# Laid-out inputs, a scan in contiguous fours and a joined 512-column stream in a two-layer attention and state-space trunk

## The chip, the cores and the metric

The kernel runs on one core of one Trainium2 chip. The metric is device time in microseconds (us) of one execution: the median of the runs shown. The engines are called PE (TensorE), PEld (its weight loads), DVE (VectorE), ACT (ScalarE), POOL (GpSimd) and SP (SyncE, which here only issues transfers).

## What is computed

The input x has 256 positions of 2048 numbers. Two layers, each:

```
h    = rmsnorm(x, pre_norm_g)
proj = h @ w_in                       # 2048 -> 6144: q, k, v, z_att, u, z_ssm
o_att = rmsnorm(diff_attention(q, k, v), subln_g) * (1 - lam_init) * silu(z_att)
y     = s5_ssm(u)                     # 64 groups of 16 channels, 64 complex states each,
                                      # h[t] = A h[t-1] + B u[t],  y = Re(C h) + D u
g     = gelu(y) @ w_glu               # 1024 -> 2048: value and gate
o_ssm = g_val * sigmoid(g_gate) * silu(z_ssm)
mix   = concat(o_att, o_ssm) @ w_out  # 2048 -> 2048
x     = x + rmsnorm(mix, post_norm_g)
```

Attention has 8 heads with two softmax maps each, a chunk-causal mask and a T5 bias table. All tensors are float32.

## The kernel before, in words

**Products in three parts.** A float32 weight tile `raw` (128 x 1024) is split into `hi`, the value rounded to fp32r by ACT (`emit_hi`, line 227), and `lo = raw - hi`, the rest, by DVE (`emit_lo`, line 245). The activations are split in the same way into `hthi` and `htlo` (later `mxhi`, `mxlo` and `ghi`, `glo`). One product is then three matmuls: hi on hi, hi on lo, lo on hi.

**Half steps.** All weights of a layer are cut into 72 chunks, in the order u (the first half as `U4`, four k groups at a time for all four column blocks; the second half as `u`), q, k, v and z_att in turns, z_ssm, w_glu, w_out. Each chunk is two half steps (hs) of one 512 KB weight tile, 288 half steps in all. The loop at line 1174 does for each half step: issue the load of half step hs + 6 (`emit_dma`, SP's queue, five buffers), start what is due (`hooks`, line 1081), round the weights of hs + 2 on ACT, let the running generators go on one step (`run_first`), compute lo of hs + 2 on DVE with other DVE work filled around it, issue the matmuls of hs (`main`, line 981), and let generators waiting for accumulators go on (`run_second`). In u, q and k the weights are the stationary operand and the activations stream, 256 columns: 24 matmuls a half step. In v, z, w_glu and w_out the activations are stationary and 512 weight columns stream: 12 matmuls a half step.

**The planner.** Each DVE helper adds an estimated cost (`cost`, line 100) to a sum. What is left of a half step's budget (`BUDS`, `BUDL`, `CAP`, lines 1141 and 1229) is given to `fill` (line 213), which takes operations from a queue (`weave`): parameters, discretisation (`z_ops`, `g_ops`), the scan.

**Start of layer 1** (the first layer; the code's l = 0). x is loaded by positions in four column pieces (line 1150), transposed on PE (`build`, line 634, four transposes for two k groups, one call per half step up to the sixth), scaled by the norm's gain and split. The sum of squares is made by ACT from x (`rstd_gen`, line 650); the row scale comes after the product, as `rbc`, when u, q, k are evacuated (`evac`, line 919).

**State space.** `prep_gen` (line 485) loads B with 8 DMAs (line 496) and C with 4 (line 501), transposes C with 16 PE transposes into `psc`, and builds the matrices for four time steps at once (z, wi, gc, the Toeplitz block t0). It runs for layer 1 from half step 2 and for layer 2 beside layer 1's w_glu stage. u goes to DRAM and comes back as U, four steps to a row (`u_store`, `u_load`, lines 680 and 684), `s_gen` (line 718) makes the inputs of 64 blocks, `scan_ops` (line 753) runs 62 sequential steps of four 128 x 64 operations on DVE, and `y_gen` (line 766) makes y, gelu and its split into `ghi`, `glo`, one fourth at a time.

```
    def scan_ops(l):                                              # line 753
        for s in range(2, 64):
            yield mul(t1, H[:, :, :, s - 1], ar) + SC
            yield mul(t2, H[:, ::-1, :, s - 1], ai)
            yield tt(t1, t1, H[:, :, :, s], ALU.add) + SC
            yield tt(H[:, :, :, s], t1, t2, ALU.add) + SC
...
            for kk in range(8):                                   # line 1014, u, q, k
                mm(o, hv[:, kk], S["hthi"][:, k], k == 0, False)
                mm(o, hv[:, kk], S["htlo"][:, k], False, False)
                mm(o, lv[:, kk], S["hthi"][:, k], False, k == 15)
```

At the very start `warm` (line 1135) keeps PE busy with products of ones until the first data are there: one call of six, one of `W1` = 1 and one of `W2` = 3.

Of the kernel before, what the change touches and what calls it, by code (L numbers as in the profile page):

```python
# [26 lines left out]
SC = 70  # L27
Y0 = (80, 77)
W1 = 1
W2 = 3  # L30
TB = 38
PG = 1
CAP = 1500.0
RES = 0.0
# [6 lines left out]
F0 = 7  # L41
EB = 400
# [5 lines left out]
NA = 2  # L48
TPS = ([(0, 1024), (1024, 1024)], [(0, 512), (512, 768), (1280, 768)])
# [7 lines left out]

@with_exitstack
def hybrid_trunk(ctx: ExitStack, tc, x, rel_bias, pre_norm_g, post_norm_g, w_in, lambda_q1, lambda_k1,
                 lambda_q2, lambda_k2, subln_g, ssm_a_re, ssm_a_im, ssm_log_dt, ssm_b_re, ssm_b_im,  # L60
                 ssm_c_re, ssm_c_im, ssm_d, w_glu, w_out, onehot, out):
# [80 lines left out]
    a4s = cp.tile([128, 2, 64], F32, name="a4s")  # L142
    cf = cp.tile([128, 2, 64], F32, name="cf")
# [17 lines left out]
    w_in_v = [w_in[l].rearrange("(k p) c -> p k c", p=128) for l in range(2)]  # L161
    w_glu_v = [w_glu[l].rearrange("(k p) c -> p k c", p=128) for l in range(2)]
    w_out_v = [w_out[l].rearrange("(k p) c -> p k c", p=128) for l in range(2)]
    chunks = []
    for l in range(DEPTH):
        chunks += [(l, "U4", n) for n in range(4)] + [(l, "u", b) for b in range(4, 8)]
        for seg in ("q", "k"):
            chunks += [(l, seg, b) for b in range(8)]
        for n in range(2):
            for seg in ("v", "za"):  # L170
                chunks += [(l, seg, 4 * n + j) for j in range(4)]
        for seg, n in (("zs", 8), ("glu", 8), ("out", 16)):
            chunks += [(l, seg, b) for b in range(n)]

# [5 lines left out]
    def emit_dma(hs):  # L180
        if hs >= 2 * NCH:
            return
        l, seg, b = chunks[hs // 2]
        h = hs % 2
        t = wp.tile([128, 1024], F32, tag="raw", name="raw")
        raw[hs] = t
        if seg in ("u", "q", "k"):
            c0 = COL[seg] + 128 * b
            src = w_in_v[l][:, 8 * h:8 * h + 8, c0:c0 + 128]
        elif seg == "glu":  # L190
            k0, c0 = 4 * (b % 2) + 2 * h, 1024 * (1 - b // 2 % 2) + 512 * (b // 4)
            src = w_glu_v[l][:, k0:k0 + 2, c0:c0 + 512]
        elif seg == "U4":
            src = w_in_v[l][:, 4 * b + 2 * h:4 * b + 2 * h + 2, COL["u"]:COL["u"] + 512]
        elif seg == "out":
            k0, c0 = 4 * (b % 4) + 2 * h, 512 * (b // 4)
            src = w_out_v[l][:, k0:k0 + 2, c0:c0 + 512]
        else:
            k0, c0 = 4 * (b % 4) + 2 * h, COL[seg] + 512 * (b // 4)
            src = w_in_v[l][:, k0:k0 + 2, c0:c0 + 512]  # L200
        tv = t.rearrange("p (k c) -> p k c", k=src.shape[1])
        if hs == 0:
            for kk in range(2):
                SY.dma_start(out=tv[:, kk], in_=src[:, kk])
        else:
            SY.dma_start(out=tv, in_=src)
# [20 lines left out]
    def emit_hi(hs, halves=False):  # L227
# [10 lines left out]
        else:  # L238
            hi = sp.tile([128, 1024], F32R, tag="hi", name="hi")
        for p in range(1 + halves):  # L240
            c = slice(512 * p, 512 * p + 512) if halves else slice(0, 1024)
            act(hi[:, c], raw[hs][:, c], AF.Copy)
        split[hs] = (hi, None)

    def emit_lo(hs, budget, halves=False):
        if hs >= 2 * NCH:
            return
        src, hi = raw.pop(hs), split[hs][0]
# [236 lines left out]
    def prep_gen(l, slots):  # L485
# [16 lines left out]
        for _ in range(4 if l else 6):  # L502
            yield
# [787 lines left out]
```

## Time and profile before

| | |
|---|---|
| median of 3 runs | 926.35 us (925.54 to 928.47) |
| profiled execution, its own time | 926.7 us |
| its span, first to last instruction | 924.9 us |
| granted TensorE clock, mean | 0.994 |
| DMA | 187,892 packets, 177.21 MB, mean 192 GB/s |

The span is 1.8 us shorter than the execution's own time. Busy time of PE is modelled from pipelined matmuls, so the spacing of matmuls says more than its share. Layers are numbered 1 and 2 here; the code has l = 0 and 1.

### The profile page before, as it was taken

To read this page: it belongs to the slowest core of one execution; us is meant where nothing else is said; L and a number is where in the kernel's file an instruction comes from. 1 tells how busy PE (TensorE), PEld (TensorE's weight loads), DVE (VectorE), ACT (ScalarE), POOL (GpSimd) and SP (SyncE) were. 2 spreads that over 40 slices of the span, in tenths; PEclk is the share of its full clock that TensorE was granted. 3 is DMA by queue.
4 is the path that set the end of the run, shared out by engine and by line. 5 is a ranking of instruction groups with operands and counts; after the bars stand their busy time and mean duration, and the time that the engine had idled before them with its cause. 6 is when DMAs were issued, how large, how long until landed. Compare 5 with 4: busy or idle time off the path is not lost.

```text
span 924.9 us, 17644 instructions
## 1 busy us (share of the span) xinstructions
PE 907.7 (98%) x6722; PEld 795.1 (86%) x6722; DVE 683.5 (74%) x1606; ACT 488.1 (53%) x881; POOL 17.2 (2%) x26
## 2 busy tenths in 40 slices
PE   9999999999999999999999999999999999999995
PEld 8999999888888788887889999997888788888884
DVE  4898686999995756877877449999966566665564
ACT  6643384455465667444468443335565655644451
POOL 3000000000000000000000000000000000000001
PEclk9999999999999999999999999999999999999998
DMA  9988656855654497576656866965556346665852
GB/s 303 209 231 244 185 165 172 278 158 168 184 155 137 126 232 243 171 249 201 215 173 193 230 175 168 246 187 165 163 156 183 115 137 203 197 210 168 291 183 91
DMA packets 187892, 177.21 MB, mean 192 GB/s; under 512 B 42550, under 2 KB 131184, under 8 KB 186912
## 3 DMA queue, kind: packets, MB, share of 16 engines
q1 hardware_dynamic: 187456, 175.96, 64.3%
q8 instruction: 53, 0.87, 0.4%
q14 instruction: 31, 0.25, 0.1%
q0 software_dynamic: 352, 0.13, 0.1%
HBM read 168.44 MB, written 7.88 MB: 191 GB/s over the span
## 4 chain that ended last, share of the span: by engine, by line
PE 87%; DVE 5%; ACT 3%; DMA 2%; SPq 1%; issue 1%; DVEq 0%; ACTq 0%
PE ac L113 79%; DVE lo L116 2%; DMA xt<-in_x_dram 1%; PE lga L113 1%; PE psy L113 1%; PE pss L113 1%; PE po L113 1%; SPq L496 1%; PE psw L97 1%; PE acu L113 1%; ACT junk L134 1%; DMA raw<-in_w_glu_dram 1%; ACT hi L134 1%; DMA raw<-in_w_in_dram 1%; ACT y L134 0%
## 5 line engine op out<-in xcount | busy, mean ns | idle before, releaser
L134 ACT ACTIVATE hi<-raw 128x1024 fp32r<-128x1024 f32 (+1 forms) x282 | 297.8, 1056 | 357.3 <-PE ac L113 272.2
L116 DVE TENSOR_TENSOR lo<-raw,hi 128x512 fp32r<-128x512 f32 (+1 forms) x401 | 359.8, 901 | 105.5 <-ACT hi L134 104.3
L113 PE MATMUL ac<-hthi,hi 128*128 128x256 f32 x736 | 211.7, 288 | 0.3 <-ACT hi L134 0.3
L113 PE MATMUL ac<-htlo,hi 128*128 128x256 f32 x736 | 209.4, 285 | 0.8 <-DVE htlo L123 0.5
L113 PE MATMUL ac<-hthi,lo 128*128 128x256 f32 x736 | 209.1, 284 | 0.6 <-DVE lo L116 0.5
L113 PE MATMUL ac<-hi,hthi 128*128 128x512 f32 x384 | 154.4, 402 | 0.0
L113 PE MATMUL ac<-lo,hthi 128*128 128x512 f32 x384 | 149.8, 390 | 0.4 <-DVE lo L116 0.4
L113 PE MATMUL ac<-hi,htlo 128*128 128x512 f32 x384 | 150.1, 391 | 0.0
L113 PEld LDWEIGHTS ac<-htlo,hi 128*128 128x128 f32 x736 | 141.8, 193 | 1.7 <-DVE htlo L123 1.7
L113 PEld LDWEIGHTS ac<-hthi,hi 128*128 128x128 f32 x736 | 141.7, 193 | 1.3 <-ACT hi L134 0.5
L113 PEld LDWEIGHTS ac<-hthi,lo 128*128 128x128 f32 x736 | 141.7, 193 | 1.2 <-DVE lo L116 1.2
L113 PE MATMUL ac<-lo,mxhi 128*128 128x512 f32 x228 | 89.0, 390 | 0.7 <-DVE lo L116 0.6
L113 PE MATMUL ac<-hi,mxhi 128*128 128x512 f32 x228 | 89.0, 391 | 0.0
L113 PE MATMUL ac<-hi,mxlo 128*128 128x512 f32 x228 | 88.7, 389 | 0.0
L113 PEld LDWEIGHTS ac<-hi,hthi 128*128 128x128 f32 x384 | 72.1, 188 | 16.1
L113 PEld LDWEIGHTS ac<-hi,htlo 128*128 128x128 f32 x384 | 72.1, 188 | 15.8
L113 PEld LDWEIGHTS ac<-lo,hthi 128*128 128x128 f32 x384 | 72.2, 188 | 14.6 <-DVE lo L116 0.8
L113 PEld LDWEIGHTS ac<-lo,mxhi 128*128 128x128 f32 x228 | 42.8, 188 | 10.3 <-DVE lo L116 1.5
L113 PE MATMUL ac<-hi,ghi 128*128 128x512 f32 x128 | 51.5, 403 | 0.0
L113 PEld LDWEIGHTS ac<-hi,mxlo 128*128 128x128 f32 x228 | 42.8, 188 | 8.9
L113 PE MATMUL ac<-lo,ghi 128*128 128x512 f32 x128 | 50.1, 391 | 0.3 <-DVE lo L116 0.3
L113 PEld LDWEIGHTS ac<-hi,mxhi 128*128 128x128 f32 x228 | 42.8, 188 | 8.9
(206 smaller groups left out, 1154.5 us busy)
## 6 DMA issues: line engine op xcount, KB each, us to landing
raw<-in_w_in_dram SPq DMA_DIRECT2D x191, 512.0 KB, 4.2
raw<-in_w_out_dram SPq DMA_DIRECT2D x64, 512.0 KB, 4.7
raw<-in_w_glu_dram SPq DMA_DIRECT2D x32, 512.0 KB, 4.3
U<-uds SPq DMA_DIRECT2D x48, 64.0 KB, 3.3
xt<-in_x_dram SPq DMA_DIRECT2D x8, 256.0 KB, 7.6
uds<-u SPq DMA_DIRECT2D x4, 512.0 KB, 6.0
pg<-in_post_norm_g_dram SPq DMA_DIRECT2D x2, 1024.0 KB, 7.1
xt<-in_x_dram SPq DMA_DIRECT2D x2, 1024.0 KB, 10.1
```

Of the source, the lines that this page charges most:

```text
L97: P.transpose(o, i, idn)
L113: P.matmul(o, lhsT=l, rhs=r, start=start, stop=stop, skip_group_check=True)
L116: V.tensor_tensor(o, a, b, op=op)
L134: A.activation(out=o, in_=i, func=f, **kw)
L496: SY.dma_start(out=bv[64 * d:64 * d + 64, a, r::2], in_=src[l].rearrange("(m r g) p c -> r g p m c", r=2, g=2)[r, d ^ r])
```

## The change

The host lays the inputs out by copies: x transposed (`xt`), the weights as 288 contiguous tiles in the order of use (`wst`), norm gains and D as columns (`vecs`), pole parameters (`poles`), B and C as the kernel wants them (`bc`), the lambdas (`lams`). The loads become plain; the transposes of layer 1's x, of C and of the parameters go. Layer 1's activations are split from the loaded transpose (`build0`), and its sum of squares is made from it with ACT squares, DVE adds and two matmuls against ones. The scan takes the four interleaved residues of the 64 steps as contiguous sixteens: three wide rounds, 15 narrow steps with the fourth power of the pole's step, three wide rounds back; for that the time index of u, H, y, ghi and glo is reordered. hthi and htlo become the two halves of one tile `ht`; in layer 2, u, q and k stream both halves, 512 columns, against the hi weights into the two halves of one accumulator, and the evacuation adds the halves. The lo subtraction is one operation of 1024 also where DVE work is filled around it. The planner's constants, the start's order and the hooks of u_store and u_load change with it.

```
-SC = 70
+SC = 57
-W1 = 1
-W2 = 3
+W0 = 18
+PS = 4
-CAP = 1500.0
+CAP = 1800.0
+JOIN = (1,)
...
+    if seg in ("u", "q", "k"):
+        return "w_in", 8 * h, 8, COL[seg] + 128 * b, 128
...
-        load[0] += 68 + n / 0.96
-        return 68 + n / 0.96
+        load[0] += 147 + n / 0.955
+        return 147 + n / 0.955
...
+        SY.dma_start(out=t, in_=wst[hs])
...
-            fill(budget / 3)
-            for p in range(2):
-                c = slice(512 * p, 512 * p + 512)
-                tt(lo[:, c], src[:, c], hf[:, c], ALU.subtract)
-                fill(budget / 3)
+            fill(budget / 2)
+            tt(lo, src, hf, ALU.subtract)
+            fill(budget / 2)
...
+        A.dma_start(out=prm, in_=vecs)
...
+        G.dma_start(out=pt[:, 512:704], in_=poles)
         G.dma_start(out=bt[0:32, 0:384], in_=onehot)
         G.dma_start(out=bt[0:32, 384:392], in_=rel_bias)
+        G.dma_start(out=bt[0:2, 512:768], in_=lams)
...
-        tpose(ps[:, 0:128], pt[:, 128:256], ident)
-        tpose(ps[:, 128:192], pt[0:64, 384:512], ident[0:64, 0:64])
...
-        tpose(ps2[:, 64:82], bt[0:18, 1408:1536], ident[0:18, 0:18])
...
+        for c in range(2):
+            SY.dma_start(out=bt[:, 1024 * c:1024 * c + 1024], in_=bc[l, :, 1024 * c:1024 * c + 1024])
...
-        for a, src in enumerate((ssm_b_re, ssm_b_im)):
-            for d in range(2):
-                for r in range(2):
-                    SY.dma_start(out=bv[64 * d:64 * d + 64, a, r::2],
-                                 in_=src[l].rearrange("(m r g) p c -> r g p m c", r=2, g=2)[r, d ^ r])
...
-                for j in range(4):
-                    tpose(ps[:, 128 * j:128 * j + 128], cv[:, a, 4 * hb + j], ident)
...
+            for d in range(2):
+                rows = slice(64 * d, 64 * d + 64)
+                put = slice(2 * a + 1, 2 * a + 5, 3) if d else slice(2 * a, 2 * a + 6, 5)
+                act(cmk[rows, :, put], ccv[rows, a].rearrange("p (i r) c -> p i r c", r=2), AF.Copy,
+                    scale=1.0 if a == 0 else -1.0)
...
+    def build0(k):
+        act(S["hthi"][:, k], S["xT"][:, k], AF.Copy, scale=pre_g[0][:, k:k + 1])
+        stt(S["htlo"][:, k], S["xT"][:, k], pre_g[0][:, k:k + 1], S["hthi"].bitcast(F32)[:, k], ALU.mult, ALU.subtract)
+
...
+            X = S["xT"].rearrange("p k c -> p (k c)")
+            sq = R(1, "sq")
+            a, b = sq[:, 0:1024], sq[:, 1024:2048]
+            act(a, X[:, 0:1024], AF.Square)
+            yield
+            for n in range(1, 4):
+                act(b, X[:, 1024 * n:1024 * n + 1024], AF.Square)
+                yield
+                tt(a, a, b, ALU.add)
+            for n in (512, 256):
+                tt(a[:, 0:n], a[:, 0:n], a[:, n:2 * n], ALU.add)
+            yield 1
+            psv = side("psv")
             for t in range(2):
-                j = tmp5("junk")
-                act(j, xt[t][:, 512 * n:512 * n + 512], AF.Square, accum_out=ssx[:, t, n:n + 1])
-            yield
+                mm4(psv[:, 2 * t:2 * t + 2], a[:, 128 * t:128 * t + 128], ones[:, 0:2], True, True)
...
+                hv = H[:, :, 4 * b0 + r:4 * b0 + 8:2]
+                act(hv[:, :, :, 16:64], psv[:, :, :, 0:48], AF.Copy)
+                act(hv[:, :, :, 1:16], psv[:, :, :, 48:63], AF.Copy)
+        weave.append(scan_ops(l))
...
+        c = slice(32 * l, 32 * l + 32)
+        ar = apow[:, 0, c, 3].unsqueeze(1).unsqueeze(3).to_broadcast([128, 2, 32, 16])
+        ai = a4s[:, :, c].unsqueeze(3).to_broadcast([128, 2, 32, 16])
+        br = a16[:, 0, c].unsqueeze(1).to_broadcast([128, 2, 32])
+        bi = a16[:, 1:3, c]
+        sct = R((3, 8)[l], "sct")
+        T, u = (sct[:, 1024 * i:1024 * i + 1024].rearrange("p (a m k) -> p a m k", a=2, m=32) for i in range(2))
+        h = [H[:, :, :, 16 * i:16 * i + 16] for i in range(4)]
+        prev = h[0]
+        for i in range(1, 4):
+            yield mul(u, prev[:, ::-1], ai)
+            yield mul(T, prev, ar)
+            yield tt(u, u, h[i], ALU.add)
+            yield tt(T, T, u, ALU.add)
+            prev = T
+        V.tensor_copy(h[3][:, :, :, 0], T[:, :, :, 0])
+        yield 140
+        for k in range(1, 16):
             t1 = scp.tile([128, 2, 32], F32, tag="sc1", name="sc1")
             t2 = scp.tile([128, 2, 32], F32, tag="sc2", name="sc2")
-            yield mul(t1, H[:, :, :, s - 1], ar) + SC
-            yield mul(t2, H[:, ::-1, :, s - 1], ai)
-            yield tt(t1, t1, H[:, :, :, s], ALU.add) + SC
-            yield tt(H[:, :, :, s], t1, t2, ALU.add) + SC
+            yield mul(t1, h[3][:, :, :, k - 1], br) + SC
+            yield mul(t2, h[3][:, ::-1, :, k - 1], bi)
+            yield tt(t1, t1, T[:, :, :, k], ALU.add) + SC
+            yield tt(h[3][:, :, :, k], t1, t2, ALU.add) + SC
+        for i in range(3):
+            p, o, n = (h[i - 1], h[i], 16) if i else (h[3][:, :, :, 0:15], h[0][:, :, :, 1:16], 15)
+            yield mul(u[:, :, :, 0:n], p[:, ::-1], ai[:, :, :, 0:n])
+            yield mul(T[:, :, :, 0:n], p, ar[:, :, :, 0:n])
+            yield tt(o, o, u[:, :, :, 0:n], ALU.add)
+            yield tt(o, o, T[:, :, :, 0:n], ALU.add)
...
-        act(hv, yv, AF.Copy)
-        tt(lv, yv, hv.bitcast(F32), ALU.subtract)
+        hv, lv = (S[n].rearrange("p (b k e i) -> p b e i k", b=8, e=4, i=4) for n in ("ghi", "glo"))
+        yv = pg.rearrange("p (i b e k) -> p b e i k", i=4, b=2, e=4)
+        for b in range(2):
+            act(hv[:, 2 * j + b], yv[:, b], AF.Copy)
+        for b in range(2):
+            tt(lv[:, 2 * j + b], yv[:, b], hv.bitcast(F32)[:, 2 * j + b], ALU.subtract)
...
+        if l in JOIN and seg in ("u", "q", "k"):
+            j = tmp("join")
+            act(j, ac[0][:, 256:512], AF.Copy)
+            yield
+            tt(j, ac[0][:, 0:256], j, ALU.add)
+            ac = [j]
...
+                if l in JOIN:
+                    mm(full, hv[:, kk], S["ht"][:, k], k == 0, False)
+                else:
+                    mm(o, hv[:, kk], S["hthi"][:, k], k == 0, False)
+                    mm(o, hv[:, kk], S["htlo"][:, k], False, False)
...
-        if s in (11, 17):
-            u_store(0 if s == 11 else 4)
-        if s in (12, 18):
-            u_load(0 if s == 12 else 4)
+        if s in (14, 19):
+            u_store(0 if s == 14 else 4)
+        if s in (15, 20):
+            u_load(0 if s == 15 else 4)
...
+        load_params()
+        raw[0] = wp.tile([128, 1024], F32, tag="raw", name="raw")
+        load_w0(0)
+        load_x(A, 0, 1)
+        load_x(A, 1, 2)
+        load_w0(1)
...
+        load_x(SY, 8, 12)
+        warm(W0)
         at(PG, params_gen())
-        at(2, prep_gen(0, (3, (1, 7), (4, 8))))
+        at(PS, prep_gen(0, (3, (1, 7), (8, 4))))
...
+                S["ht"] = rp.tile([128, 16, 2, 256], F32R, tag="ht", name="ht")
+                S["hthi"], S["htlo"] = S["ht"][:, :, 0], S["ht"][:, :, 1]
...
+                    for k in range(2):
+                        build0(k)
+                        emit_hi(0, True, (k,))
+                        emit_lo(0, 0, True, (k,))
+                    main(0, part=0)
+                    emit_hi(1)
+                    emit_lo(1, 0)
...
-            bal = min(bal, CAP) + (BUDL if not l and s >= 44 else BUDS[l]) + pload[0] - load[0] - 1130
+            bal = min(bal, CAP) + (2880.0 if s < 48 else 2724.0) - SPARE[2 if l else int(s >= 44)] + pload[0] - load[0] - LOT
             load[0] = 0.0
-            emit_lo(hs + 2, 0 if s >= SX else min(bal, EB) if s < F0 else bal - RES)
-            bal -= max(0.0, load[0] - 1130)
+            emit_lo(hs + 2, 0 if s >= SX else bal)
+            bal -= max(0.0, load[0] - LOT)
```

## Rows read from the trace of the kernel before

**Rows 1.** The page, busy us (share of the span) and instructions of each engine.
```profile
PE 907.7 (98%) x6722; PEld 795.1 (86%) x6722; DVE 683.5 (74%) x1606; ACT 488.1 (53%) x881; POOL 17.2 (2%) x26
```
**Rows 2.** The page, the chain that ended last, share of the span by line.
```profile
PE ac L113 79%; DVE lo L116 2%; DMA xt<-in_x_dram 1%; PE lga L113 1%; PE psy L113 1%; PE pss L113 1%; PE po L113 1%; SPq L496 1%; PE psw L97 1%; PE acu L113 1%; ACT junk L134 1%; DMA raw<-in_w_glu_dram 1%; ACT hi L134 1%; DMA raw<-in_w_in_dram 1%; ACT y L134 0%
```
**Rows 3.** The same chain in order of time: start us, us, what.
```profile
47.25 0.44 PE psc L97 x4
...
65.70 46.25 PE ac L113 x384
...
357.67 21.78 PE ac L113 x96
```
**Rows 4.** Windows: A:B us, PE, PEld, DVE, ACT, POOL busy (x), clock, DMA, GB/s.
```profile
7.33:27.30 19.97, 18.96 (x148) 17.46 (x148) 12.42 (x24) 15.98 (x42) 2.35 (x3) 1.00 0.96 293
...
555.00:621.00 66.00, 66.00 (x552) 66.00 (x551) 63.11 (x208) 24.41 (x23) 0.00 (x0) 1.00 0.76 201
```
**Rows 5.** Timeline of PE up to 7.4 us: start us, us, what.
```profile
1.06 2.93 PE L113 MATMUL warm<-ones 128*128 128x128 f32 x12 [1.06 <-DVE sso L1147]
...
4.15 0.80 PE L113 MATMUL warm<-ones 128*128 128x128 f32 x2
...
6.20 0.83 PE L113 MATMUL warm<-ones 128*128 128x128 f32 x6
7.33 0.39 PE L113 MATMUL ac<-hthi,hi 128*128 128x256 f32 x1 [0.30 <-ACT hi L134]
```
**Rows 6.** DMA issues: count, KB each, median us from issue to landing.
```profile
raw<-in_w_in_dram SPq DMA_DIRECT2D x2, 256.0 KB, 4.4
```
**Rows 7.** Windows of PE, tile ac, then acu: us, busy (x), clock, DMA, GB/s.
```profile
7.30:50.75 43.45, 32.41 (x240) 1.00 0.99 263
7.30:50.75 43.45, 6.34 (x48) 1.00 0.99 263
```
**Rows 8.** PE groups by form, 7.3 to 50.75 us: busy us, mean ns, idle before.
```profile
L97 PE MATMUL psx<-ident,xt 128*128 128x128 f32 x24 | 3.7, 277 | 0.0
L97 PE MATMUL psc<-ident,cn 128*128 128x128 f32 x16 | 2.4, 273 | 0.0
```
**Rows 9.** Waits of PEld, 7.3 to 50.75 us: total us, times, longest us.
```profile
PEld ac L113 <- DVE lo L116: 1.2, 3, 0.5
PEld ac L113 <- DVE htlo L123: 1.0, 2, 0.7
PEld ac L113 <- ACT hi L134: 0.5, 1, 0.5
```
**Rows 10.** PE groups, 323 to 354 us; chain, 322 to 352; PEld waits, 316 to 352.
```profile
L97 PE MATMUL psc<-ident,cn 128*128 128x128 f32 x16 | 2.4, 274 | 0.2 <-DMA cn<-in_ssm_c_re_dram 0.2
...
by line: SPq L496 25.0%; PE ac L113 18.6%; DMA raw<-in_w_glu_dram 17.9%; issue 12.4%; SPq L501 10.0%; DVE lo L116 4.1%; ACT hi L134 3.7%; ACT bt L134 2.1%; ACT mxhi L134 1.6%; PE psc L97 1.5%; ACT cm L134 1.3%; SPq L206 1.3%; PE psf L97 0.7
...
PEld ac L113 <- DVE lo L116: 1.5, 2, 0.8
PEld psc L97 <- PE ac L113: 0.6, 1, 0.6
```
**Rows 11.** Groups by form, whole span: busy us, mean ns, idle before, releaser.
```profile
L116 DVE TENSOR_TENSOR lo<-raw,hi 128x1024 fp32r<-128x1024 f32 x161 | 196.0, 1222 | 90.8 <-ACT hi L134 90.3
...
L116 DVE TENSOR_TENSOR H<-sc,sc 128x64 f32<-128x64 f32 x124 | 33.6, 271 | 1.9
...
L116 DVE TENSOR_TENSOR gc<-bt,apow 128x1024 f32<-128x1024 f32 x8 | 9.8, 1220 | 0.0
...
L123 DVE SCALAR_TENSOR_TENSOR k<-ac,rbc 128x256 f32<-128x256 f32 x16 | 6.7, 420 | 5.4 <-PE ac L113 5.4
...
L134 ACT ACTIVATE rbc<-psr 128x256 f32<-128x256 f32 x2 | 0.7, 374 | 0.0
```
**Rows 12.** Chain in order of time, 735 to 741 us: start us, us, what.
```profile
735.53 1.09 ACT ghi L134
```
**Rows 13.** Waits of PEld, 424 to 431 us: total us, times, longest us.
```profile
PEld ac L113 <- DVE lo L116: 1.5, 2, 1.0
```

More of the change, by code (lines that the diff above doesn't have):

```diff
@@ L40 @@
 PD = (1, 1)
-F0 = 7
-EB = 400
 W3 = 4
@@ L158, in hybrid_trunk @@
     subg = [prm[:, 48 + l:49 + l] for l in range(2)]
[L161 to L173, printed above, removed]
+    chunks = _chunks()
     NCH = len(chunks)
@@ L225, in fill, with emit_hi @@
                 weave.popleft()
-    def emit_hi(hs, halves=False):
+    def emit_hi(hs, halves=False, parts=(0, 1)):
         if hs >= 2 * NCH:
@@ L616, in g_ops @@
         for hf in range(2):
+            while hf and f"cmfree{l}" not in S:
+                yield 100
             gc = R(gslots[hf], "gc")
@@ L718, in s_gen @@
     def s_gen(l):
-        yield from until(f"wi{l}")
+        yield from until(f"wa{l}")
         H = rp.tile([128, 2, NPAIR, 64], F32, tag="big", name="H")
@@ L724, in s_gen @@
         for b0 in range(0, 8, 2):
-            while b0 >= 4 and not S["u2"]:
+            while b0 >= 4 and not (S["u2"] and f"wi{l}" in S):
                 yield
@@ L979, in evac, with main @@
         yield
-    def main(hs, only=None):
+    def main(hs, only=None, part=None):
         i, h = divmod(hs, 2)
@@ L985, in main @@
         if seg == "U4":
-            if i % LAYER == 0 and h == 0:
+            if i % LAYER == 0 and h == 0 and not part:
                 S["acc"] = [acc(f"ac{j}") for j in range(4)]
@@ L1003, in main @@
             else:
-                for kk in range(2):
-                    for j in range(4):
-                        one(kk, j)
+                for kk in range(2) if part is None else (part,):
+                    for pr in (None,) if part != 0 else range(3):
+                        for j in range(4):
+                            one(kk, j, pr)
             done = b == 3 and h == 1
@@ L1265, in _onehot, with _lay, pairs @@
     return o
+def _lay(np, x, pre_norm_g, w_in, w_glu, w_out, lambda_q1, lambda_k1, lambda_q2, lambda_k2, subln_g, ssm_a_re, ssm_a_im,
+         ssm_log_dt, ssm_b_re, ssm_b_im, ssm_c_re, ssm_c_im, ssm_d, **rest):
+    lay = {"xt": x[0].T.reshape(16, 128, 256).transpose(1, 0, 2)}
+    w = {"w_in": w_in, "w_glu": w_glu, "w_out": w_out}
+    hs = []
+    for l, seg, b in _chunks():
+        for h in range(2):
+            name, k0, nk, c0, nc = _half(seg, b, h)
+            hs.append(w[name][l].reshape(-1, 128, w[name].shape[2])[k0:k0 + nk, :, c0:c0 + nc]
+                      .transpose(1, 0, 2).reshape(128, 1024))
+    lay["wst"] = np.stack(hs)
+    col = lambda a: a.reshape(-1, 128).T
+    lay["vecs"] = np.concatenate([col(pre_norm_g), col(ssm_d), col(subln_g)], axis=1)
+    def pairs(a):
+        a = a.reshape((2, 32, 2) + a.shape[2:]).copy()
+        a[:, 1::2] = a[:, 1::2, ::-1]
+        a = np.moveaxis(a, 1, 3)
+        return a.reshape((2, 128) + a.shape[3:])
+    dt = np.repeat(ssm_log_dt[:, :, None], 64, axis=2)
+    lay["poles"] = np.stack([np.moveaxis(pairs(a), 0, 1).reshape(128, 64) for a in (ssm_a_re, ssm_a_im, dt)], axis=1)
+    lay["poles"] = lay["poles"].reshape(128, 192)
+    lay["lams"] = np.concatenate([lambda_q1, lambda_k1, lambda_q2, lambda_k2], axis=1)
+    cs = [np.swapaxes(a, 2, 3) for a in (ssm_c_re, ssm_c_im)]
+    lay["bc"] = np.stack([pairs(a) for a in (ssm_b_re, ssm_b_im, *cs)], axis=2).reshape(2, 128, 2048)
+    lay["onehot"] = _onehot(np)
+    return lay
 def kernel(**inputs):
```

246 lines of the change are left out of this document (105 added, 141 removed).

## The prediction

> **What bounds the kernel now.** I read the page's busy shares first: TensorE (PE) works 98% of the span, VectorE (DVE) 74%, ScalarE (ACT) 53% [rows 1]. Busy PE is not PE at its peak, so the second view is the chain that ended last: 79% of it is the weight matmuls of line 113 [rows 2]. The third is the same chain in order of time, which gives the price of one matmul where nothing interrupts: 384 with 256 columns take 46.25 us, 120.4 ns each; 96 with 512 columns take 21.78 us, 226.9 ns each [rows 3]. The stretch 555 to 621 us shows what this means for the other engines: 552 matmuls in 66.0 us, 119.6 ns each, so PE runs at that pace without a gap while DVE is busy 63.1 us of the 66 [rows 4]. A full DVE costs nothing there. Time can be won in three ways only: fewer or longer PE instructions, an earlier first weight matmul, fewer waits of PE. I go through the change by these.
>
> **The time to sum against.** The profiled execution took 926.7 us, 0.35 above the median of 926.35; the sum is made on 926.7 and 0.35 taken off. About 0.3% (2.8 us) is what a measurement can tell from no change.
>
> **The first weight matmul.** It starts at 7.33 us, released by ACT's rounding of the first weights [rows 5]. The change puts 18 warm-up matmuls on PE's queue ahead of it, and one warm-up is two instructions: 36. The first 12 took 2.93 us, 0.244 us each; the 6 just before the first weight matmul took 0.83 us, 0.138 each [rows 5], so the pace halves between. The slow ones last until somewhere between 4.95 us, the end of the last slow pair, and 6.20, the start of the fast six; taking 5.5, there are (5.5 - 1.06)/0.244 = 18 slow ones, then 18 at about 0.11 (six less their tail), 2.0 us: PE is free at 7.5. I take 7.45, a loss of 0.1. The data should be there: a 256 KB half of the first weights took 4.4 us to land [rows 6], now issued first of all on SP, at about 0.8 us, so 5.2, and its halves are rounded within 1.2 us. Bounds: 0.5 earlier, 0.8 later. The parameter DMA and two x loads now issue on ACT ahead of its table load; ACT's first needed result moves to about that landing, so their issue time is covered. POOL issues 4 small loads in place of 11, and nobody queues behind the missing ones.
>
> **The start, 7.33 to 50.75 us.** Here stand 240 + 48 = 288 weight matmuls [rows 7], 34.6 us at 120 ns, in 43.4 us: 8.8 us lost. The groups say to what [rows 8]: 24 transposes of x and 16 of C, in groups of four that cost 0.44 us each [rows 3], so 6 x 0.44 = 2.6 and 4 x 0.44 = 1.8; named waits of PE's weight load for lo, htlo and hi, 1.2 + 1.0 + 0.5 = 2.7 [rows 9]; the remaining 1.7 are the small parameter transposes and matmuls. After: the x transposes go (2.6), the C transposes go (1.8), three of the parameter transposes go (about 0.6) and two thin matmuls that sum the squares over partitions come (about 0.4): 0.2. Of the waits I let half go, 1.3. What they hang on is DMA and DVE: the C and B loads of 12 DMAs become 2, x comes once and in pieces as it is needed, the weights lie contiguous, but DVE gets work. It was busy 12.4 of the 20.0 us from 7.33 to 27.3 [rows 4]; adding the squares costs three 1024-wide adds at 1.22 (as a lo) [rows 11] and two narrower ones, about 4.8 us, which makes 17.2 of 20. It fits without room; what is late next is htlo or lo of the following half step. Bounds for the waits: all 2.7 gone, or 2 us more. ACT does four squares of 1024 for eight of 512: no more than before. Sum of the stretch: 2.6 + 1.8 + 0.2 + 1.3 = 5.9.
>
> **Layer 2's preparation, 323 to 354 us.** The other 16 C transposes stand here [rows 10], 4 x 0.44 = 1.8 us. Their data makes further loss: the 12 DMAs of lines 496 and 501 hold SP's queue (35% of that stretch's chain is their issue), the next w_glu load lands after them, and PE waits for the lo made of it [rows 10]. PE's waits in 316 to 352 are up to 1.5 us on lo (longest 0.8) and 0.6 at the transposes. I take 0.6 of the first and 0.4 of the second: 2.8 in all, bounds 1.8 to 3.9. The four ACT copies that now fill cm from the loaded C replace 16 pairs from PSUM.
>
> **u, q and k of layer 2 as one 512.** 20 blocks of 16 row groups: 320 times, two matmuls of 256 become one of 512. 2 x 120.4 - 226.9 = 13.9 ns, times 320: 4.5 us. The third matmul, lo weights on 256 columns, stays. The two halves must then be added: one ACT copy of 256 (0.37, as rbc) and one DVE add (0.42, as k from the accumulator) per block [rows 11], 7.5 and 8.4 us, beside PE: ACT is busy 24 of 66 us there [rows 4], and DVE is freed by the scan. The copy waits on ACT's queue for the block's last matmul, with the rounding for hs + 2 and its lo behind it, which have two half steps, 5.6 us, until their use. The evacuation comes one half step later; four accumulators, of which a block holds one for four half steps, leave one spare. Without that cover each block would cost its 0.8 us once, 16 us. By the Trainium skill, TensorE: Matmul & The Clock Gate, section Back-to-back issue gap, a warm stream spaces matmuls by columns over 2.4 GHz plus about 2.5 ns; by that two of 256 are only 2.6 ns dearer than one of 512, and this term would be an estimated 0.8 us. The rows disagree (120.4 and 226.9, both 13 to 14 ns above streaming), and the measurement decides.
>
> **The scan.** Per layer 62 steps of four 64-wide operations, each about 0.27 us [rows 11], become 24 operations of 1024 elements (1.22, as gc) and 15 steps of four: 62 x 4 x 0.27 = 67 us of busy time becomes 29 + 16 = 45. On PE nothing: in 555 to 621 us, where DVE is fullest, PE already has its full pace [rows 4]. The cover is PE itself. What it buys is room for the joins.
>
> **Costed at nothing.** ghi and glo written in two pieces and another order: 8 times 1.09 us on ACT; once, at 735.5 us, a ghi stands on the chain ahead of the attention's copies and PE's po [rows 12], so between 1 us better and 1 worse. u_store and u_load (1 + 8 DMAs a half) move two or three half steps later past as many weight loads on SP: those go out sooner, six half steps ahead of use, and the state matmuls that read U wait for the transposed weights (psw) anyway. The lo in one piece of 1024 for two of 512, and planner constants: they set only what DVE does in its free time. Both activation parts in one tile: both were released by neighbouring matmuls.
>
> **Sum.** -0.1 + 5.9 + 2.8 + 4.5 = 13.1: 926.7 - 13.1 = 913.6, less 0.35: 913.3 us.
>
> **Rivals.**
> (a) The start doesn't shrink: DVE, now full there, and the loads give back what the transposes freed; of 5.9 only 1.9 remains. For: 17.2 of 20 us on DVE. Against: the lost instructions are PE's own and don't return. 917.3 us.
> (b) The join buys nothing: in the pair the next weights' load hides behind only 256 columns, and where it falls behind, the pair costs 361 ns as three of 256 do. For: 119.6 ns with the loader busy 66.0 of 66.0 us [rows 4]. Against: in today's form every load hides behind 256 columns, and the new pair gives each second one more. 917.8 us. The rule of the skill cited above would come near it, by another way: 917.0.
> (c) Slower: the wide scan operations delay lo. Each holds DVE 1.22 us, and up to two stand ahead of a lo. It happened at 424 to 431 us, where 1.2-us operations around lo made PE's weight load wait 1.5 us [rows 13]; both layers have 24 such operations on gc and ztmp, so about 0.06 each. The two scans have 48. From 0.27 us each they eat the 13.1; at 0.4 they cost 19, and the time is 913 + 19 = 932. Against: at the measured 0.06 it is 3 us, and lo is made two half steps ahead.
>
> **How the numbers follow.** Forecast 0.70; (a) 0.14; (b) 0.08; (c) 0.06; the rest 0.02. The best sum (all start waits gone, 1.4 more; 0.6 more at the start; preparation 1.1 more; ghi 1) is near 909; the worst of the known bounds (start 3.3 less, late first matmul 0.7, preparation 1.0, ghi 1) near 919. The range 908.5 to 919 takes in (a) and (b), and leaves out (c) and the tails. Faster by over 0.3%: all but most of (c) and part of the rest, 0.92; within: 0.03; slower: 0.05.
>
> **What would show it.** Right: no psx until layer 2 and no psc; the first weight matmul at 7.2 to 7.7 us; the 288th weight matmul done by 45 us; in layer 2's q and k, pairs at 347 ns, so 24 former matmuls in 2.78 us where it was 2.89; PE waiting nowhere over 1 us but at the layer border. Wrong: waits of PE for lo in the scan's stretches, for htlo in the first 30 us, or a pair over 355 ns. The whole is wrong if PE's lost time outside the parts named grows by over 5 us.

## The result, and the profile after

The changed kernel takes 934.3 us (median of 4 runs, 933.0 to 934.7) against 926.9 before (4 runs): ratio 1.0077, 95% interval 1.0057 to 1.0097. It is **slower**; the forecast was 913.3 us and faster. The profiled execution took 934.7 us with a span of 933.0; the mean granted clock fell from 0.994 to 0.987.

The first lines of the page after answer to [rows 1]: busy time and instructions of each engine, the granted clock in 40 slices, the DMA total.

```profile
PE 905.2 (97%) x6354; PEld 778.5 (83%) x6354; DVE 672.1 (72%) x1202; ACT 486.4 (52%) x878; POOL 13.7 (1%) x19
...
PEclk9999999999999999999999999999999999999998
...
DMA packets 65069, 176.11 MB, mean 189 GB/s; under 512 B 17574, under 2 KB 24512, under 8 KB 64096
```

PE has 368 instructions fewer, DVE 404 fewer, the DMA a third of the packets. Every engine is busy for less time and the kernel takes longer: the loss is in waits of PE. A second view, windows at six places of after (us, PE, PEld, DVE, ACT, POOL busy, granted clock, DMA share, GB/s), shows what became of them:

```profile
7.98:10.10 2.12, 0.28 (x3) 0.08 (x1) 0.49 (x2) 1.06 (x3) 0.00 (x0) 1.00 1.04 409
10.90:14.30 3.40, 3.40 (x16) 3.40 (x17) 3.26 (x5) 3.40 (x7) 0.00 (x0) 0.50 1.04 413
38.20:41.60 3.40, 3.40 (x17) 3.40 (x18) 3.26 (x17) 0.00 (x0) 0.00 (x0) 0.50 0.40 143
55.30:58.70 3.40, 3.40 (x18) 3.40 (x17) 1.47 (x5) 0.35 (x1) 0.00 (x0) 0.50 0.35 94
475.10:478.50 3.40, 3.40 (x19) 3.40 (x18) 2.77 (x5) 2.27 (x5) 0.00 (x0) 0.50 0.33 84
533.10:536.60 3.50, 3.50 (x62) 3.09 (x53) 0.00 (x0) 1.20 (x4) 0.00 (x0) 0.51 0.58 233
```

In the first PE stands still. In the other five it works without a gap at half clock, 1.2 of 2.4 GHz, so a stretch of 3.4 us costs up to 1.7 us of work. Each came after a wait of PE of 1.5 to 3 us. Before, there was one such stretch away from the tail, 3.4 us at 469.7 us, after the layer border; here are five.

Where the time went is read best from the start times of the half steps. This table is worked out from the starts of the weight matmuls in three traces (us); the third kernel, "repaired", is the seventh experiment below.

| stretch | before | after | repaired | forecast gain |
|---|---|---|---|---|
| up to the first weight matmul | 7.33 | 6.57 | 7.43 | -0.1 |
| half steps 0 to 14 | 52.14 | 57.68 | 48.31 | 5.9 |
| 15 to 46 | 103.77 | 105.21 | 103.77 | 0 |
| 47 to 78 (layer 1's scan) | 98.05 | 100.38 | 98.03 | 0 |
| 79 to 110 (layer 2's preparation) | 109.83 | 107.23 | 106.93 | 2.8 |
| 111 to 142 | 91.39 | 90.11 | 90.11 | 0 |
| 143 to 190 (border, layer 2's u, q, k) | 155.97 | 159.72 | 151.99 | 4.5 |
| 191 to the end | 306.42 | 306.10 | 306.03 | 0 |
| span | 924.9 | 933.0 | 912.6 | 13.1 |

The preparation gave what was forecast. The start lost 5.5 us, layer 2's u, q, k lost 3.8, and two stretches costed at nothing lost 3.8. The start's 5.5 is one execution's: in three profiles of the experiments below that leave the start as it is (1, 5 and 6), half steps 0 to 14 took 56.3, 55.9 and 52.6 us. The last has both 2.1 us waits named next and no half clock there; so the waits alone take away the forecast gain, and the clock makes the loss.

**The start after.** The chain that ended last, in order of time (start us, us, what):

```profile
35.34 1.24 DVE sq L140
...
36.60 0.70 DVE sq L140
...
37.32 0.43 DVE sq L140
...
37.80 0.67 PE psv L137 x4
38.47 13.06 PE acu L137 x96
51.54 0.45 PE psr L137 x2
...
52.01 0.39 ACT rbc L158
...
52.87 1.04 DVE u L140 x2
```

The two thin matmuls `psv` (sum of squares over partitions, four instructions) stand in PE's queue and wait for DVE's adds. The row scale made of them (`psr`, `rbc`) comes at 51.5 us; before, psr stood at 36.8 us. Without `rbc` no block of `U4` can be evacuated (copied out of its accumulator), so its four accumulators are held and the next product waits. The waits of PE in 26 to 60 us (total us, times, longest us):

```profile
PE ac L137 <- DVE u L140: 2.1, 1, 2.1
PE psv L137 <- DVE sq L140: 2.1, 1, 2.1
```

Ahead of these stands the wait of the first window above. ACT's timeline (start us, us, what; in brackets the idle time before it and what ended that) names it: the second piece of x, which the change issues on ACT's own queue.

```profile
5.49 0.51 ACT L158 ACTIVATE ht<-xT,prm 128x256 fp32r<-128x256 f32 x1 [1.85 <-DMA xT<-in_xt_dram]
5.91 0.61 ACT L158 ACTIVATE hi<-raw 128x512 fp32r<-128x512 f32 x1
9.04 0.51 ACT L158 ACTIVATE ht<-xT,prm 128x256 fp32r<-128x256 f32 x1 [2.52 <-DMA xT<-in_xt_dram]
```

The first piece was used 4.3 us after its issue at 1.2 us, the second 7.4 us after its own at 1.65. The page's DMA issues (count, KB each, median us from issue to landing) have one figure for both:

```profile
xT<-in_xt_dram ACTq DMA_DIRECT2D x2, 128.0 KB, 7.3
```

**Layer 2 after.** The same chain from 508 to 535 us. The state matmuls `pss` read U, which goes to DRAM (`uds`) and back:

```profile
507.84 0.44 PE psw L121 x4
...
522.22 4.84 DMA uds<-u
...
527.12 0.33 SPq L687
...
530.32 2.25 DMA U<-uds
...
532.76 1.69 PE pss L137 x62
534.45 3.96 PE ac L137 x16
```

The last psw is done at 508.3, and U comes 24 us later. PE stands in `pss` at the end of that, 2.8 and 1.6 us (waits of PE, 515 to 545 us: total us, times, longest us):

```profile
PE pss L137 <- DMA U<-uds: 4.4, 2, 2.8
```

### The profile page after: what moved, and what is told of

Same layout as the page of the kernel before. It is cut to its first block, busy times and chain, and to the rows that moved or that the text cites. A ratio compares the mean times of both kernels' runs of the same rounds, so it can differ in the third digit from the quotient of the medians.

```text
span 933.0 us, 16359 instructions
## 1 busy us (share of the span) xinstructions
PE 905.2 (97%) x6354; PEld 778.5 (83%) x6354; DVE 672.1 (72%) x1202; ACT 486.4 (52%) x878; POOL 13.7 (1%) x19
## 4 chain that ended last, share of the span: by engine, by line
PE 87%; DVE 6%; ACT 2%; DMA 2%; issue 1%; SPq 0%; ACTq 0%; DVEq 0%
PE ac L137 77%; PE acu L137 3%; DVE lo L140 2%; PE lga L137 1%; PE po L137 1%; PE psy L137 1%; DMA xT<-in_xt_dram 1%; PE pss L137 1%; DVE H L140 1%; PE psw L121 1%; ACT hi L158 1%; DVE sct L140 1%; DMA uds<-u 1%; DVE sq L140 1%; ACT y L158 0%
## 5 line engine op out<-in xcount | busy, mean ns | idle before, releaser
L140 DVE TENSOR_TENSOR lo<-raw,hi 128x1024 fp32r<-128x1024 f32 (+1 forms) x282 | 342.7, 1218 | 128.1 <-ACT hi L158 126.5
L137 PE MATMUL ac<-ht,hi 128*128 128x256 f32 (+1 forms) x1120 | 259.5, 318 | 4.3 <-DVE u L140 2.1
L137 PE MATMUL ac<-hi,ht 128*128 128x512 f32 x768 | 249.3, 396 | 0.0
L137 PEld LDWEIGHTS ac<-ht,hi 128*128 128x128 f32 x1120 | 187.4, 194 | 19.1 <-ACT hi L158 4.5
L137 PE MATMUL ac<-ht,lo 128*128 128x256 f32 x704 | 200.7, 286 | 0.6 <-DVE lo L140 0.6
L137 PEld LDWEIGHTS ac<-hi,ht 128*128 128x128 f32 x768 | 144.2, 188 | 31.5
L137 PE MATMUL ac<-lo,ht 128*128 128x512 f32 x384 | 150.3, 391 | 1.5 <-DVE lo L140 1.4
L137 PE MATMUL ac<-hi,mx 128*128 128x512 f32 x456 | 141.9, 390 | 0.0
L137 PEld LDWEIGHTS ac<-ht,lo 128*128 128x128 f32 x704 | 136.3, 194 | 1.1 <-DVE lo L140 1.1
L137 PE MATMUL ac<-lo,mx 128*128 128x512 f32 x228 | 88.7, 389 | 0.0
```

The source lines that it names most:

```text
L137: P.matmul(o, lhsT=l, rhs=r, start=start, stop=stop, skip_group_check=True)
L140: V.tensor_tensor(o, a, b, op=op)
```

## The experiments

Each is a small edit of the changed kernel. Times are medians; the ratio is to the kernel before on the same chip (927.05 to 927.5 us). What a run takes "off the changed kernel" is counted from the 934.3 us of the result. The first five repair one wait each. One thing blurs their medians, so that the profiles have to tell the parts: which of the waits is followed by a half clock differs between executions.

**1. Layer 2's u goes out as early as it did** (half steps 11, 12, 18, 19 in layer 2 only; before the change 11, 12, 17, 18).

```
-        if s in (14, 19):
+        if s in ((14, 19), (11, 18))[l]:
-        if s in (15, 20):
+        if s in ((15, 20), (12, 19))[l]:
```

> The changed kernel with u_store and u_load of layer 2 alone put back (store at half steps 11 and 18, load at 12 and 19; the second pair one later than before, since the joined evacuation is one later). Theory T1: in layer 2 the transposed weights are long ready, so s_gen starts at half step 15 and PE's first state matmuls wait for the U that is loaded in that same half step: PE stands 2.8 + 1.6 us at 528 to 533 us, and the granted clock is halved for 3.4 us after it. Then both waits go, the half clock goes, and the time falls by 5 to 6 us, to about 929. Rival: the transfer through DRAM itself became slower beside the new weight stream; then the waits stay at over 2 us and the time stays within 2 us of 934.

Measured: 926.76 us (10 runs, 922.4 to 929.4), ratio 0.9987 (0.9970 to 1.0005): 7.5 us off the changed kernel. Its chain in layer 2:

```profile
514.47 11.30 PE ac L137 x64
525.76 1.09 PE pss L137 x64
526.85 3.02 PE ac L137 x16
529.87 1.09 PE pss L137 x64
530.96 14.33 PE ac L137 x80
```

Both waits are gone (`pss` is 1.09 us of work) and so is the half clock behind them: half steps 151 to 166 took 51.1 us where it was 57.3. The half clock at the border was absent in this execution too, 1.5 us, and so was that near 55 us, though nothing there was touched.

**2. The sum of squares from half step 1 on, not 3.**

```
-        if s == (1 if l else 3):
+        if s == 1:
```

> The changed kernel with layer 1's sum of squares started at half step 1 instead of 3, as before the change. Theory T2: the sum comes too late: psv stands in PE's order two half steps after its last square, PE waits 2.2 us for DVE's adds near 35 us, the row scale comes late, the four accumulators of the first u are held until it is there, and PE waits 2.2 us again near 52 us; each wait is followed by 3.4 us at half clock, 1.7 us of work each. Then both waits and both half-clock stretches go: 2 x 2.2 + 2 x 1.7 = 8, about 926. Rival: DVE is simply too full in the first 50 us (three 1024-wide adds on top); then the waits move to lo or htlo between 15 and 40 us and the time stays within 3 us of 934.

Measured: 929.9 us (5 runs), ratio 1.0036 (1.0013 to 1.0060). `psr` moved from 51.4 to 47.3 us and the wait of U4's accumulators is gone. But `psv` now waits 3.2 us for DVE's adds, and the half clock behind it is twice as long (windows):

```profile
32.20:39.00 6.80, 6.75 (x31) 6.75 (x32) 4.66 (x19) 0.58 (x1) 0.00 (x0) 0.50 0.52 160
```

So half the remedy: the sums must be early, and the matmuls that read them must stand later on PE's queue.

**3. The first two x pieces on SP's queue, in the order of use.**

```
+        load_x(SY, 0, 1)
         load_w0(0)
-        load_x(A, 0, 1)
-        load_x(A, 1, 2)
+        load_x(SY, 1, 2)
         load_w0(1)
```

> The changed kernel with the first two pieces of x issued on SP, in the order of need (piece 0, first half of the first weights, piece 1, second half), instead of on ACT. Theory T3: a 128 KB piece on ACT's queue takes 7.3 us to land because it shares the transfer engines with 1.5 MB that SP has queued meanwhile; PE stands 2.1 us at 8 us and then 3.4 us at half clock. In SP's order piece 1 lands by 5 us: the 2.1 us and most of the 1.7 go, 2 to 4 us less, 930 to 932. Rival: all loads share the engines whatever queue they are on; then piece 1 still lands after 8 us and the time stays at 934.

Measured: 932.24 us (10 runs, 928.3 to 935.4), ratio 1.0056 (1.0039 to 1.0073). ACT's timeline:

```profile
3.24 0.51 ACT L158 ACTIVATE ht<-xT,prm 128x256 fp32r<-128x256 f32 x1 [0.57 <-DMA prm<-in_vecs_dram]
...
5.57 0.51 ACT L158 ACTIVATE ht<-xT,prm 128x256 fp32r<-128x256 f32 x1 [1.16 <-DMA xT<-in_xt_dram]
```

The second piece is rounded at 5.6 us in place of 9.0. Half step 0 takes 4.0 us instead of 6.5, and the half clock at 10.9 is gone: half step 15 starts 3.7 us earlier. Not all of that is the edit's. Of the six profiles with these pieces on ACT's queue, three have the half clock near 11 us and three (experiments 4 to 6) don't, and the one at 38.2 is missing here though its wait of 2.1 us is still there. The median gained 2.1; later clock drops took the rest (this profile has 6.8 us at half clock at 526).

**4. Urgent work of the planner goes alone.** `fill` takes an urgent operation and then, if budget is left, also one of the common queue. Here urgent operations go alone as long as any is queued.

```
-            if not weave or budget <= 0:
+            if urgent or not weave or budget <= 0:
```

> The changed kernel with one line of the filler changed: while urgent small operations are queued, they go alone, instead of each taking one operation of the ordinary queue with it. Theory T4: near 249 to 257 us the scan's 1024-wide operations ride along with the urgent ones, two 1.13 us operations to a lo, which is 3.6 us of DVE in a half step of 2.72, and PE waits for lo three times, 1.8 us in all. Then these waits go, 1.5 to 2 us less than the changed kernel (934), about 932.5; the row scale of layer 1 may also come earlier and save part of the 2.2 us wait near 52 us. Rival: the wide operations block lo whoever lets them in (the prediction's rival c); then the waits only move to other places of the scan and the sum of PE's waits for lo stays near 1.8 us.

Measured: 926.97 us (10 runs, 925.3 to 931.4), ratio 1.0007 (0.9992 to 1.0023): 7.3 us off, far more than either theory gave it. It was meant for rival (c)'s waits, lo behind wide scan operations in layer 1's scan. In the kernel after they are these (waits of PE's weight load, 244 to 260 us):

```profile
PEld ac L137 <- DVE lo L140: 2.8, 4, 1.0
```

They are gone here, and half steps 47 to 78 take 98.13 us, as before (98.05). The larger part the expectation had named only as a possibility: the row scale's own short operations are urgent work too, and each had a common one beside it. Its chain at the start:

```profile
36.53 0.61 PE psv L137 x4
37.14 10.22 PE acu L137 x72
47.37 0.43 PE psr L137 x2
47.80 2.87 PE acu L137 x24
50.67 9.36 PE ac L137 x78
```

From `psv` to `psr` it is 10.8 us where it was 13.7, `psr` stands one half step further ahead, so that PE has the last matmuls of `acu` (the two `u` blocks after `U4`) to do meanwhile, and no wait and no half clock follow near 52 us. This profile also has no half clock at 10.9, which the edit does not explain: its first weight matmul came at 8.0 us, after which the late x piece cost nothing. Only the median says that the gain is more than such luck.

**5. The state matmuls start at `wi`, not at `wa`**: after all transposed weights, as before the change, not after the first half of them. After, layer 1 has short waits at the state matmuls (waits of PE, 140 to 156 us):

```profile
PE pss L137 <- ACT H L158: 1.0, 2, 0.7
```

```
-        yield from until(f"wa{l}")
+        yield from until(f"wi{l}")
```

> The changed kernel with s_gen waiting for all transposed weights again, not for the first half. Theory T5: starting the state matmuls between the second half's transposes makes four kinds of accumulators share the four side banks, and PE waits 0.9 + 0.4 us for ACT's copies at 149 to 151 us of layer 1; then they go, 1.3 us less, about 933. The scan starts some 10 us later in layer 1, and its end may delay y. Rival: the wait is the state matmuls' own; then it stays.

Measured: 933.74 us, ratio 1.0069 (1.0050 to 1.0088). The waits are gone and half steps 15 to 46 take 103.77 us, as before. The median gained 0.6, no more than such runs scatter.

**6. Without the join.**

```
-JOIN = (1,)
+JOIN = ()
```

> The changed kernel without the join: u, q and k of layer 2 stream 256 columns three times again and are evacuated without the addition. As predicted the join is worth 320 x 13.9 ns = 4.5 us on PE: 24 matmuls go from 2.77 back to 2.88 us a half step. u is then evacuated one half step earlier, so the wait for U in layer 2 is as long, or shorter by up to 2 us. Theory: 936 to 939. Rival (the join's copy, add and later evacuation eat its gain): 932 to 934.

Measured: 937.22 us (4 runs, 934.0 to 939.0), ratio 1.0107 (1.0085 to 1.0129): the join is worth 2.9 us here, by medians that the clock blurs. Number 8 prices it without that.

**7. All five repairs, and `psv` two half steps later on PE's queue.** The five edits above together, and in the sum of squares:

```
             for n in (512, 256):
                 tt(a[:, 0:n], a[:, 0:n], a[:, n:2 * n], ALU.add)
+            yield
+            yield
             yield 1
             psv = side("psv")
```

> All repairs together: u_store and u_load of layer 2 early, the sum of squares from half step 1 with its matmuls two half steps later behind it, the first two pieces of x on SP, urgent operations alone, s_gen after all transposed weights. If the three long waits with their half clock are what the change costs, their parts add: 934.3 less 6 (U), 8 (row scale), 3 (x), 1.8 (lo), 1.3 (banks) gives 914, with 911 to 918 as its range, near the 913.3 that was predicted for the change itself. Rival: the start stays bound by loads and DVE, whatever the order; then the waits move within the first 40 us and the time is 918 to 923.

Measured: 914.93 us (4 runs, 914.5 to 915.9), ratio 0.9866 (0.9851 to 0.9880): as expected, 19.4 us off the changed kernel and 12 off the one before. The page of its profile, and its chain at the start:

```profile
PE 896.0 (98%) x6354; PEld 771.9 (85%) x6354; DVE 674.1 (74%) x1202; ACT 487.8 (53%) x878; POOL 13.7 (2%) x19
```

```profile
34.88 0.34 PE psv L137 x4
35.23 8.74 PE acu L137 x72
43.96 0.43 PE psr L137 x2
44.40 2.87 PE acu L137 x24
47.27 12.84 PE ac L137 x107
```

`psv` is now 0.34 us, without a wait, and nothing stands behind `psr`. Windows of half steps 0 to 14, first of this kernel, then of the one after:

```profile
7.43:55.74 48.31, 46.18 (x373) 44.69 (x372) 42.27 (x106) 29.96 (x42) 0.00 (x0) 1.00 0.78 263
```

```profile
6.57:64.25 57.68, 51.23 (x373) 49.20 (x372) 42.80 (x108) 29.79 (x43) 0.00 (x0) 0.91 0.66 229
```

The same work of PE, DVE and ACT, 9.4 us apart. Three waits of 1.9, 2.1 and 2.1 us and three stretches at half clock (3 x 1.7) make 11.2; number 7 has two waits left, 2.0 us in sum, on DVE's half of `ht`: 9.2. The later place of `psv` was tried only together with the rest. DVE's 42.3 of 48.3 us is no obstacle. The layer border's wait of 1.5 us is still there, at 459.0 us, and here no half clock follows it.

**8. Number 7 without the join.** Edit: `JOIN = ()`.

> The repaired kernel without the join. On the repaired kernel nothing else waits in layer 2's u, q and k, so the difference to it is the join alone: 4.5 us more by the prediction's 320 x 13.9 ns (4.0 to 4.9). Rival: the copy, the add and the later evacuation give back 2 us or more; then 2.5 us or less.

Measured: 916.92 us (916.8 to 917.1), ratio 0.9886 (0.9871 to 0.9900). The join is worth 2.0 us by medians, 2.5 by the spans (915.1 and 912.6), not 4.0 to 4.9. It also says what the rest of the change is worth with its waits repaired: about 10.1 us of 927.05.

**9. Number 7 with the scan step by step again**, on the new order of time: 62 steps of four 64-wide operations, entered in the planner at 190 (125 for the second of four).

```
+        for s in range(2, 64):
+            p, q = 16 * ((s - 1) % 4) + (s - 1) // 4, 16 * (s % 4) + s // 4
...
+            mul(t1, H[:, :, :, p], ar)
...
+            mul(t2, H[:, ::-1, :, p], ai)
...
+            tt(t1, t1, H[:, :, :, q], ALU.add)
...
+            tt(H[:, :, :, q], t1, t2, ALU.add)
```

> The repaired kernel with the scan again in 62 sequential steps of four 64-wide operations, on the new time order, each operation entered in the planner at 190 (125 for the second of four), so that it ends in time for y. By the prediction the scan in fours gives PE nothing, because PE is already at its pace beside a full DVE: within 1.5 us of the repaired kernel's 914.9. Rival 1: the wide operations still cost PE waits for lo (the prediction's rival c); then the sequential scan is faster, 911 to 913. Rival 2: the sequential scan fills DVE so far that lo, the joins or y come late; then 917 to 922.

Measured: 917.46 us (916.4 to 917.8), ratio 0.9892 (0.9878 to 0.9907). The scan in fours is a gain, 2.5 us by medians and 1.9 by spans, where the prediction had nothing and its rival (c) a loss. Part of it is in layer 1's scan, where DVE gives lo later (waits of PE's weight load, 225 to 260 us; in number 7 half steps 47 to 78 took 98.03 us, here 99.53):

```profile
PEld ac L137 <- DVE lo L140: 1.0, 3, 0.6
```

**10. Number 7 with the join in both layers.** Edit: `JOIN = (0, 1)`.

> The repaired kernel with the join in both layers. In the repaired kernel the join of layer 2 was worth 2.0 us by the medians and 2.5 by the profiles: 19 of its 40 half steps ran at 2.83 us instead of 2.77, until a wait of PE ended that state, and one new wait for lo cost 0.5. If layer 1 behaves alike, 912 to 913. By the prediction's 13.9 ns a pair it would be 910.4. Rival: in layer 1 DVE and ACT are full with the parameters in the same half steps, the later evacuation of u holds its accumulators, and the gain is lost in waits: 915 or more.

Measured: 914.82 us (913.4 to 915.6), ratio 0.9864 (0.9847 to 0.9881): nothing measurable. The pairs do get shorter, layer 1's half step 47 starts 9.2 us earlier than in number 7. But by half step 79 the lead is 3.9 us and by 191 it is 1.0: the state matmuls `pss` that PE did in half steps 15 to 46 come in 47 to 78, and y comes late for w_glu (waits of PE, 312 to 332 us):

```profile
PE ac L137 <- ACT ghi L158: 1.6, 2, 1.0
PE ac L137 <- DVE glo L140: 1.1, 2, 0.8
```

**11. Number 7 with half of the warm-up matmuls**, `W0 = 9` for 18.

> The repaired kernel with 9 warm-ups instead of 18. In the repaired kernel the first weight matmul starts at 7.4 us, when the warm-ups end, though its data are rounded by 4.6. With 9 it starts near 5.1; but the second half of the first weights is rounded only at 8.2 and the second weights at 10, so PE waits there instead, and half step 1 still starts near 10.4: 914 to 916. If the waits let the clock fall for 3.4 us, 1.7 more. Rival: the start is bound by the warm-ups; then 2 us less, 912 to 913.

Measured: 915.83 us (914.5 to 917.0), ratio 0.9872 (0.9854 to 0.9890): no gain. The first weight matmul starts at 4.9 us, but PE then waits for x and weights, half step 1 starts at 10.28 in place of 10.43, and this comes behind (windows):

```profile
12.00:15.40 3.40, 3.40 (x19) 3.40 (x18) 3.40 (x6) 3.22 (x6) 0.00 (x0) 0.50 1.04 424
```

Number 7 is the version to keep: it beats both kernels, and 9 to 11 don't improve on it.

## Why the prediction was wrong

**What held.** That PE bounds the kernel and that its own removed instructions are gained: the preparation gave 2.6 us for 2.8, and with the waits repaired the start gave 3.8. That scan work on DVE costs PE little, though not nothing: the new scan gains some 2 us (experiment 9). The gains stand in the changed kernel; more than all of them was lost to waits that the sum had not got, or had at nothing, and to the clock behind them. That number 7 came so near to the forecast, 914.9 for 913.3, is in part luck: the start and the join gave some 4 us less than forecast, and 1.3 us at [rows 13] and 1.5 at the border came in that nobody had forecast.

**A step that failed: "u_store and u_load ... move two or three half steps later", costed at nothing, because "the state matmuls that read U wait for the transposed weights (psw) anyway".** That holds in layer 1, where the chain has the last psw done at 150.0 us and the next pss at 151.3. In layer 2 the matrices are made a stage ahead, psw ends at 508 us and U comes at 532. The cover named for layer 1 was carried over to a layer that has none. Experiment 1: 7.5 us by medians; by its half steps 6.2 us in 151 to 166, of which the waits are 4.4 us and the half clock up to 1.7.

**The term that failed most: the start, 5.9.** In the profiled execution it was 5.5 the other way. Three things were missing in it.
- The **row scale**. The change moves its source from ACT's squares of x (done early, off PE) to a chain through DVE and two matmuls on PE's queue, behind which the weight matmuls stand. I counted its adds as 4.8 us of DVE's busy time in 7.33 to 27.3 us and its matmuls as 0.4 us, and didn't ask when the last one is due: the adds ran at 29.3 to 37.8 us, behind that stretch. The block evacuations hang on it: psr at 51.4 us for 36.8. Two waits, 2.1 us each (experiments 2, 4 and 7).
- The **queue of the first x pieces**: "so 5.2, and its halves are rounded within 1.2 us" was for the weights on SP; x on ACT's queue I costed by its issue time alone. The second piece landed at 9 us. In five other profiles with this part unchanged it was rounded at 8.4 to 9.7 us, with experiment 3's and number 7's order at 5.6 and 5.2.
- The **planner**. "planner constants: they set only what DVE does in its free time". `fill` takes an urgent operation together with a common one, and the dearer operations of the scan and the urgent chain of the row scale both ran in that way. Experiment 4 alone took 7.3 us off the median, part of it clock.

The first weight matmul came at 6.57 us, earlier than the forecast's bounds allow. In the eleven profiles with 18 warm-up matmuls it came at 6.5 to 8.0 us, the later the later the granted clock rose (4.0 to 7.2 us); the 5.5 us that the prediction took is where it rose in the trace of before.

**A part that stands nowhere in the prediction:** the change also starts layer 1's state matmuls at `wa`; half steps 15 to 46 lost 1.4 us, which experiment 5 gives back.

Rival (a) gave the start's loss to a full DVE. Number 7 does the same DVE work in 9.4 us less: order, not load.

**Rival (c), at 0.06, is no explanation of the size.** Its mechanism is there (lo behind wide operations at 244 to 260 us, PE's weight load waits 2.8 us in sum and PE 1.4, gone in experiment 4). For the 24 wide operations of layer 1's scan 2.8 us is 0.12 each, twice the price of [rows 13], and not the 0.4 us that it needed. It gave 932 us, near what came, by luck. In the other direction the wait of [rows 13] itself is gone after the change, 1.3 us in half steps 111 to 142, a gain that the forecast had not.

**What was priced nowhere: the clock.** I added waits at their own length. In the kernel after, each of the three long waits of the start and the pair in `pss` was followed by 3.4 us at half clock: four stretches more than before (the border had its own in both), 1.7 us of work each, 6.8 us, where the span grew by 8.1. The Trainium skill, TensorE: Matmul & The Clock Gate, section What's actually happening, names two states of TensorE's clock, 2.4 GHz when it has been busy and 1.2 when it has been idle; the windows above agree (1.00 and 0.50). That the half clock follows waits as short as these is shown by the runs, not by that section. The forecast drew on the same page and gave the clock no price. Not each wait is followed by it: of the eleven waits of 2.1 us in the starts of all profiles seven were; the 1.1 us waits in number 7 were not, and the border's 1.5 us was in the kernel before and was not in number 7.

**The join, 4.5, was mis-sized:** 2.0 to 2.5 (experiment 8). The spacing forecast for a pair, 347 ns, is reached, but not everywhere. By the starts of its half steps, a joined half step, eight times a matmul of 512 columns and one of 256, takes either 2.83 us (354 ns for the two) or 2.77 (347), against 2.88 unjoined. In number 7 the pace is 2.83 up to half step 170 and 2.77 from 172 on; the switch comes at a wait for a lo at 551 us, which is new and makes half step 171 0.6 us longer. 20 half steps at 0.055 us above the forecast pace make 1.1 us and the wait 0.6, which leaves 2.8; the remaining 0.3 to 0.8 is not assigned. Rival (b) named the mechanism "the pair costs 361 ns"; that was not seen. By the rule of the Trainium skill that the prediction cites, the term would have been an estimated 0.8 us: the measurement lies between it and the rows, but the spacing is that of the rows. The section gives that rule for single matmuls and not for a stream of weight loads and matmuls, which this kernel is; the prediction left that out, and by its own figures the 2.6 ns should be 2.5.

## What to carry to other kernels

A cover has to be looked up for each layer and stage where the moved step runs: ask what the reader of the moved data waits for *there*. For a short chain whose result releases many (a row scale, a normalisation), the sum of its busy times says nothing; write down when its last operation is due, what else stands in the same queues, and keep matmuls that read it out of PE's queue until the data are there. And price a new wait of PE of 2 us at up to 4 where the trace shows half clock behind such waits.

## What was not expected of the hardware

- **Two paces of the joined stream in one and the same code.** Ten profiles have joined half steps in layer 2. All begin at 2.83 us, and all have in half step 171 the same wait for lo, 0.36 to 0.42 us of PE. Behind it five run at 2.77 us and five at 2.83, to the end of k, about 1 us apart. In experiment 2 the pace was 2.77 already in half steps 162 to 164, behind the waits in pss, and 2.83 again in 169 and 170, with only other matmuls and no wait between. What sets the pace was not found; the traces show that it can change at a pause of PE, not at each, and once without one.
- **A small load on a queue with little else can be slow**: the second 128 KB piece on ACT's queue was used 7.4 us after its issue, beside SP's loads of weights and x; in SP's own order the same piece was rounded 3.5 us sooner.
- **Half clock came in pieces of 3.4 us, sometimes of 6.8** (away from the tail), after waits of 1.3 to 4.6 us, and in experiment 11 after several of 0.6 to 0.9; after like waits it is sometimes missing. Executions of one kernel with waits of 2 us and more lie 7 us apart (experiments 1 and 3, 10 runs each); those of numbers 7 to 10, whose longest wait is the border's 1.5 us, lie 0.3 to 2.2 apart (4 runs each).
